# Queries and keys of an attention unit in four transfers, both heads together, in place of eight

## The chip, the core and the metric

The kernel runs on one core of one Trainium2 chip, in one launch. The metric is the device time of an execution in microseconds. Three runs of the kernel before gave 2951.26, 2949.39 and 2949.75 us, a median of 2949.75 us. A fourth execution was recorded by the hardware profiler; every view below is of that one.

## What is computed

One decoder layer on 2048 tokens of width 1024, in float32. Cut to the part that the change touches, with 64 columns per head, 8 heads of each kind:

```python
proj = h @ w_in[l]                                   # h: normalised, modulated tokens
q_f, k_f, v_f, q_s, k_s, v_s, f_logit = jnp.split(proj, offsets, axis=-1)
o_fox = forgetting_attention(...)                    # softmax(q.k/8 + F[t] - F[s]) v, s <= t
o_sb = stick_breaking_attention(...)                 # sigmoid(z) * prod(1 - sigmoid(z)) v, s < t
mix = jnp.concatenate([head_rms_norm(o_fox, ...), head_rms_norm(o_sb, ...)], axis=-1)
x = x + gate_a * (mix @ w_out[l])                    # then a gated MLP and a last norm
```

## The kernel before, in words

Products run on TensorE with each float32 operand split into a coarse part and a rest (`split`, L44 to L46, writes both), so a product is two or three matmuls.

The attention works in 32 **units** in a fixed order: first the stick-breaking kind (`sb`), then the forgetting kind (`fox`); in each, four pairs of heads; in each pair, four blocks of 512 queries. A unit's work grows with its block: block 0 of a `fox` pair is short, block 3 long. Two things run side by side in program order, mixed by `interleave`: `attend` for unit i (logits at L596 and L597, transposes of the weights at L606, their split copies at L610 and L611, the weighted values at L615), and `project`, which runs ahead and makes the queries, keys and values of later units.

A projection (`proj`) loads eight tiles `hp` of 512 KB, one for each 128 rows of the width, from DRAM (`hs`, L468), multiplies them with the query and key weights (L342), and writes the split queries and keys of the unit to DRAM (`qk_...`, L380 and L394). Every other pair also makes values (L413), which go to DRAM as `vs_...` (L440). There are ten `hp` buffers. They are also used for the loads of the late modulation (L776) and of the output weights (L746, L753), which run in the same stretch.

When unit i+1 is projected, `load_unit` brings its tiles from DRAM to SBUF while unit i is attended. `Q` is 128 partitions by 2 heads by 2 parts by 512 queries; the 64 columns of a head stand on partitions 0 to 63 and again on 64 to 127. `K` is 128 partitions by 2 heads by 512 keys; its lower 64 partitions hold the coarse part and its upper 64 the rest. A matmul over all 128 partitions thus sums two products. In DRAM the unit is `src`, 128 rows (head, then column) by 2 (queries, keys) by 2 parts by 512, so a row is 8 KB. There are two `Q` buffers and five each of `K` and `V`: the queries of unit i+1 can be fetched only when the last logits of unit i-1 are done, while keys of a pair stay for all its later blocks.

Nearly all transfers of this part, in and out, are issued by the SP queue, one after another: a transfer that waits (for a buffer, or for data) holds back all that stand behind it. The SP transfers take eight semaphores in turn, and each also waits until the transfer that used its semaphore before has landed. The order of the instructions on each engine is set by the scheduler of the framework before the run; the program gives it only the dependences and a few fixed places.

Of the kernel before, what the change touches and what calls it, by code (L numbers as in the profile page):

```python
# [21 lines left out]
HD = 64  # L22
# [12 lines left out]
def kernel(ctx: ExitStack, tc: tile.TileContext, x, c, w_ada, b_ada, g_attn, w_in, b_fgate,  # L35
                      g_out_fox, g_out_sb, w_out, g_mlp, w_up, conv_w, conv_b, w_down, g_final, out):
    nc = tc.nc
# [3 lines left out]
    def f(t):  # L41
        return t.bitcast(F32)
# [179 lines left out]
    rows = sm.tile([NR, P], F32, name="rows")  # L222
    begin_block(0)
    for r, src in ((R_GA, g_attn), (R_GM, g_mlp), (R_GF, g_out_fox), (R_GS, g_out_sb), (R_BA, b_ada)):
        n = src.shape[1] // P
# [121 lines left out]
    def unit_tiles():  # L347
        Q = sb.tile([P, 2, 2, TB], F32R, name="Q", tag="Q", bufs=2)
        K = sb.tile([P, 2, TB], F32R, name="K", tag="K", bufs=5)
        V = sb.tile([P, 4, 2, P], F32R, name="V", tag="V", bufs=5)  # L350
        return Q, K, V

    def load_unit(kind, p, tb, res):
        if (kind, p) == ("sb", 0):
            return
        Q, K, V = unit_tiles()
        src = qs.pop((kind, p, tb))
        for h in range(2):
            rows = slice(h * HD, (h + 1) * HD)
            for r in range(2):  # L360
                half = slice(r * HD, (r + 1) * HD)
                nc.sync.dma_start(f(Q[half, h]), src[rows, 0])
                nc.sync.dma_start(f(K[half, h]), src[rows, 1, r])
        nc.sync.dma_start(f(V), vs[kind][p][tb])
        res.append((Q, K, V))

# [459 lines left out]
    def attend_steps(u):  # L826
        kind, p, tb = u
        if kind == "fox":
            return sum(2 * (2 + 2 * tb + j2 + 1) for j2 in range(2)) + 1
        return sum(2 * (tb + 1 + 2 * tb + j2 + 1) for j2 in range(2)) + 1  # L830
# [189 lines left out]
    weights["sb", 0], results["sb", 0] = load_w("sb", 0), []  # L1020
    first_block(weights["sb", 0])
    load_unit(*units[0], results["sb", 0])
    loaded_units = [1]
    close_pool("mod")
# [5 lines left out]
    for i, u in enumerate(units):  # L1030
# [10 lines left out]
        n = attend_steps(u)  # L1041
# [16 lines left out]
        def follow(m):  # L1058
            while projected[0] < goals[min(m, n - 1)]:
                with tc.issue_after(marks[max(0, len(marks) - 1 - LAG)]) if START <= i < ENDQ else nullcontext():  # L1060
                    if next(ahead, 1) is not None:
                        break
            if nxt and projected[1] > i + 1 and loaded_units[0] == i + 1:
                loaded_units[0] += 1
                load_unit(*nxt, results[nxt[:2]])
# [10 lines left out]
    def chunk(u, c):  # L1076
        t, n, q = ORDER.get(u, TURN)[c]
        if (t, n) not in banks:
            banks[t, n] = bank(psc, "bc", 2) if u == 1 and t == 0 else bank(psd, "o", 4)
        with fixed():  # L1080
            out_matmuls(u, banks[t, n], t, n, q)
        return t, n, q
# [213 lines left out]
    for u in range(1, NU):  # L1296
        for c in range(8 if u == 1 else 0, 16):
            t, n, q = chunk(u, c)
# [386 lines left out]
    for i in range(7):  # L1685
        nxt = {}
        kept = []
        for s in range(2):
# [4 lines left out]
            if left:  # L1693
                half, n = lefts[i]
# [68 lines left out]
```

## Time and profile before

| | |
|---|---|
| median of 3 runs | 2949.75 us |
| the profiled execution, its own time | 2943.39 us |
| its span, first to last instruction | 2941.4 us |
| TensorE busy in the span | 2867.8 us (97%) |
| VectorE, ScalarE, GpSimd busy | 2179.5, 1686.0, 901.1 us |
| moved by the DMA engines | 601.89 MB, mean 205 GB/s |
| attention units | about 220 to 1480 us of the span |
| gated MLP, end | about 1480 to 2941 us |

The span is read as a sequence of stages. A view of groups gives the busy time of an engine by source line; the view of waits says which instruction waited, and for whom; the view by stretches gives for any piece of the span the busy time of each engine, the granted TensorE clock (PEclk, 1.00 is full), the busy share of the DMA engines, and the GB/s that they moved. PE is the matmuls of TensorE, DVE VectorE, ACT ScalarE, POOL GpSimd, SP the queue that issues transfers. Tiles are named without their buffer numbers, with the line of the kernel before.

### The profile page before, as it was taken

The numbers are of one execution on the slowest core, as the hardware profiler recorded it, in microseconds if no ns is written. First come the engines' busy times: TensorE is split into PE (matmuls) and PEld (weight loads), VectorE is DVE, ScalarE is ACT, GpSimd is POOL, SyncE is SP. The second block draws the span as 40 slices with busy tenths as digits, with TensorE's granted clock in tenths as the row PEclk, the third lists the DMA queues.
The fourth block names the chain that finished last, engine by engine and source line by source line (L and its number), as shares of the span: only waits on it lengthen the run. The fifth ranks groups of instructions, "written<-read, shape, count | busy, mean of one in ns | idle before, by whom it ended". The sixth has DMA issues, their size and how long they took to land.

```text
span 2941.4 us, 45922 instructions
## 1 busy us (share of the span) xinstructions
PE 2867.8 (97%) x15772; PEld 2459.7 (84%) x15772; DVE 2179.5 (74%) x3464; ACT 1686.0 (57%) x3187; POOL 901.1 (31%) x967
## 2 busy tenths in 40 slices
PE   8999999999999999999999999999999999999998
PEld 7888888888988988888888788888788888888887
DVE  5787778877886656658843788888998888575476
ACT  5776767677776656658744554444444445433342
POOL 0431322243032423231213344444254543142200
PEclk8999999999999999999999999999999999999999
DMA  9749756867469794794537775554754444975644
GB/s 293 255 139 321 236 188 207 301 211 229 162 212 356 269 277 139 232 323 140 182 120 233 245 232 128 130 136 129 236 132 125 130 130 132 309 257 185 216 158 151
DMA packets 348346, 601.89 MB, mean 205 GB/s; under 512 B 34672, under 2 KB 178800, under 8 KB 348112
## 3 DMA queue, kind: packets, MB, share of 16 engines
q1 hardware_dynamic: 324208, 558.06, 57.7%
q0 software_dynamic: 10880, 20.97, 4.3%
q10 hardware_dynamic: 13024, 19.93, 1.9%
q8 instruction: 124, 2.03, 0.3%
q14 instruction: 110, 0.90, 0.1%
HBM read 420.77 MB, written 177.02 MB: 203 GB/s over the span
## 4 chain that ended last, share of the span: by engine, by line
PE 46%; DMA 3%; DVE 2%; SPq 1%; ACT 1%; issue 1%; POOL 0%; DVEq 0%; ACTq 0%; POOLq 0%
PE ps_o L1315 19%; PE ps_t L1315 7%; PE ps_o L1614 6%; PE ps_t L1614 3%; PE ps_bc L1614 3%; PE ps_o L912 1%; PE ps_pv L615 1%; DMA r<-rstd 1%; PE ps_bc L912 1%; PE ps_pt L606 1%; PE ps_o L1609 1%; DMA wo<-wos 1%; DMA hm<-hf_m 1%; SPq L895 1%; DVE op L46 1%
## 5 line engine op out<-in xcount | busy, mean ns | idle before, releaser
L1315 PE MATMUL ps_o<-op,wu 128*128 128x512 f32 x2592 | 608.0, 389 | 2.0 <-DVE snap L1366 1.5
L1315 PEld LDWEIGHTS ps_o<-op,wu 128*128 128x128 f32 x2592 | 486.2, 188 | 103.9 <-DVE snap L1366 1.9
L611 DVE TENSOR_TENSOR at<-ps_pt,at 128x512 fp32r<-128x512 f32 (+1 forms) x576 | 366.1, 652 | 100.2 <-ACT at L610 97.3
L636 DVE TENSOR_TENSOR_SCAN a<-r,a 128x512 f32<-128x512 f32 (+2 forms) x320 | 368.3, 1167 | 77.8 <-ACT a L631 39.9
L342 PE MATMUL ps_pj<-hp,w_qk 128*128 128x512 f32 x1512 | 411.2, 403 | 14.5 <-DMA hp<-hs 12.9
L610 ACT ACTIVATE at<-ps_pt 128x512 fp32r<-128x512 f32 (+1 forms) x576 | 318.5, 576 | 139.1 <-PE ps_pt L606 123.1
L615 PE MATMUL ps_pv<-at,V 128*128 128x256 f32 x2216 | 386.8, 292 | 9.3 <-DVE at L611 4.2
L615 PEld LDWEIGHTS ps_pv<-at,V 128*128 128x128 f32 x2216 | 320.9, 190 | 39.8 <-DVE at L611 11.4
L342 PEld LDWEIGHTS ps_pj<-hp,w_qk 128*128 128x128 f32 x1512 | 275.4, 190 | 71.0 <-DMA hp<-hs 16.2
L45 ACT ACTIVATE wu<-wuraw 128x512 fp32r<-128x512 f32 x204 | 128.9, 632 | 248.5 <-PE ps_o L1315 190.1
L596 PE MATMUL ps_qk<-K,Q 128*128 128x512 f32 (+2 forms) x640 | 265.7, 416 | 5.6 <-ACT a L631 3.3
L413 PE MATMUL ps_pj<-w_v,hp 128*128 128x256 f32 (+1 forms) x1536 | 236.6, 288 | 2.1 <-DVE hp L422 1.6
L597 PE MATMUL ps_qk<-K,Q 128*128 128x512 f32 (+2 forms) x640 | 235.7, 369 | 0.0
L1315 PE MATMUL ps_t<-op,wu 128*128 128x512 f32 x888 | 220.8, 390 | 1.0 <-DVE op L46 1.0
L413 PEld LDWEIGHTS ps_pj<-w_v,hp 128*128 128x128 f32 x1536 | 209.0, 189 | 10.9 <-DVE q L373 1.5
L630 ACT ACTIVATE r<-ps_qk 128x512 f32<-128x512 f32 (+2 forms) x320 | 173.1, 541 | 58.2 <-PE ps_qk L597 55.5
L46 DVE TENSOR_TENSOR wu<-wuraw,wu 128x512 fp32r<-128x512 f32 x204 | 189.6, 930 | 18.1 <-ACT wu L45 16.7
L1315 PEld LDWEIGHTS ps_t<-op,wu 128*128 128x128 f32 x888 | 166.4, 188 | 36.5 <-DVE op L46 1.8
L606 PE MATMUL ps_pt<-edge,a 128*128 128x128 f32 x1088 | 185.1, 274 | 8.4 <-DVE a L636 7.8
L1614 PE MATMUL ps_o<-op 128*128 128x512 f32 x840 | 191.5, 389 | 0.0
L1614 PEld LDWEIGHTS ps_o<-op 128*128 128x128 f32 x840 | 157.7, 188 | 32.7
L679 ACT ACTIVATE p<-p,mn 128x128 f32<-128x128 f32 (+15 forms) x128 | 153.9, 1203 | 53.3 <-DVE mn L675 52.2
(342 smaller groups left out, 5237.6 us busy)
## 6 DMA issues: line engine op xcount, KB each, us to landing
hp<-hs SPq DMA_DIRECT2D x224, 512.0 KB
wuraw<-in_w_up_dram SPq DMA_DIRECT2D x80, 512.0 KB
ra<-g SPq DMA_DIRECT2D x136, 256.0 KB
rb<-in_w_down_dram SPq DMA_DIRECT2D x108, 256.0 KB
g<-u SPq DMA_DIRECT2D x80, 256.0 KB
hs<-hp SPq DMA_DIRECT2D x32, 512.0 KB
hp<-in_w_ada_dram SPq DMA_DIRECT2D x32, 512.0 KB
qk_fox<-q SPq DMA_DIRECT2D x32, 512.0 KB
```

The lines of the kernel that those rows point to most:

```text
L46: (lo_engine or nc.gpsimd).tensor_sub(lo, src, f(hi))
L342: nc.tensor.matmul(acc, w[kt][:, a, n], h[:, bb], start=kt == 0 and i == 0, stop=kt == KT - 1 and i == 2)
L413: nc.tensor.matmul(av[:, t * width:(t + 1) * width], hts[kt][:, a, tok], w[1][kt][:, bb, 0:width], start=kt == 0 and m == 0, stop=kt == KT ...
L596: nc.tensor.matmul(b[:, :cw], Q[:, hl, 0, qcols], K[:, hl, :cw], start=True, stop=False)
L597: marks.append(nc.tensor.matmul(b[:, :cw], Q[:, hl, 1, qcols], K[:, hl, :cw], start=False, stop=True).ins)
L606: nc.tensor.transpose(b[:, i * P:(i + 1) * P], blk(kts[kk], qi), ident)
L610: copies = [nc.scalar.activation(at[:, 0, lo:], b[:, lo:], AF.Copy).ins, nc.vector.tensor_sub(at[:, 1, lo:], b[:, lo:], f(at[:, 0, lo:])).ins]
L611: nc.vector.tensor_sub(at[:, 1, lo:], b[:, lo:], f(at[:, 0, lo:])).ins]
L615: m = nc.tensor.matmul(o[:, 0:2 * P], V[kt // 4][:, kt % 4, hl, :], rhs, start=first and kk == 0 and w == 0, stop=last and kk == 1 and w == 1)
L636: nc.vector.tensor_tensor_scan(rev, r[:, 0:need][:, ::-1], rev, 0.0 if right[qi] is None else right[qi][:, 0:1], ALU.mult, ALU.add)
L1315: nc.tensor.matmul(b, w[:, p, j], o[:, q], start=first and i == 0, stop=last and i == 2, skip_group_check=True)
L1614: nc.tensor.matmul(b, a[:, p, t * P:(t + 1) * P], w[:, q], start=first and i == 0, stop=last and i == 2, skip_group_check=True)
```

## The change

Only `load_unit` changes. For a unit, the kernel before issues four transfers for `Q` (256 KB each, one head onto one half of the partitions) and four for `K` (128 KB each). The changed kernel issues two for each, one for each half of the partitions, that carry both heads: 512 KB and 256 KB, with three-dimensional patterns (64 partitions, 2 heads, one contiguous run). The program text names the keys first. The bytes, the contiguous runs (4 KB for Q, 2 KB for K) and the destinations stay as they were. 28 of the 32 units load this way, so 224 transfers become 112.

```diff
-        for h in range(2):
-            rows = slice(h * HD, (h + 1) * HD)
-            for r in range(2):
-                half = slice(r * HD, (r + 1) * HD)
-                nc.sync.dma_start(f(Q[half, h]), src[rows, 0])
-                nc.sync.dma_start(f(K[half, h]), src[rows, 1, r])
+        for r in range(2):
+            half = slice(r * HD, (r + 1) * HD)
+            nc.sync.dma_start(f(K[half]), src[:, 1, r].rearrange("(h d) n -> d h n", h=2))
+        for r in range(2):
+            half = slice(r * HD, (r + 1) * HD)
+            nc.sync.dma_start(f(Q[half]), src[:, 0].rearrange("(h d) s n -> d h s n", h=2))
         nc.sync.dma_start(f(V), vs[kind][p][tb])
```

The scheduler sees other transfers, and so it also orders other instructions anew. On TensorE the order is the same up to about 239 us of the span of before; it differs by places of up to about 7 us of matmul work from there to about 480 us and from 800 to about 1340 us, and is the same again behind that, through the whole MLP. Three places follow. In a name such as `qk_fox_1_9353` the first number is the block of 512 queries, and `hs_2` is the third of the eight `hp` tiles of a projection.

**First place, SP, at the change from the `sb` units to the `fox` units.** The Q transfer here is that of block 1 of the first `fox` pair. Before (the next row is the load of `hs_2`):

```order
L440 DMA vs_fox_3_217<-q_10929 128x1024
L753 DMA wos_175<-hp 256x1x512
L746 DMA hp<-in_w_out_dram 128x1024
L363 DMA K<-qk_fox_3_10634 64x512
L753 DMA wos_175<-hp 256x1x512
L364 DMA V<-vs_fox_1_215 128x1024
L363 DMA K<-qk_fox_3_10634 64x512
L440 DMA vs_fox_3_221<-q_10930 128x1024
L363 DMA K<-qk_fox_3_10634 64x512
L362 DMA Q<-qk_fox_1_9353 64x1024 x4
L363 DMA K<-qk_fox_3_10634 64x512
L364 DMA V<-vs_fox_2_216 128x1024
```

And in the change, from the same point of the program:

```order
L746 DMA hp<-in_w_out_dram 128x1024
L753 DMA wos_175<-hp 256x1x512
L440 DMA vs_fox_3_217<-q_10877 128x1024
L360 DMA K<-qk_fox_3_10582 64x2x512
L753 DMA wos_175<-hp 256x1x512
L440 DMA vs_fox_3_221<-q_10878 128x1024
L360 DMA K<-qk_fox_3_10582 64x2x512
L364 DMA V<-vs_fox_1_215 128x1024
L468 DMA hp<-hs_2_62 128x1024
L363 DMA Q<-qk_fox_1_9309 64x2x1024 x2
L468 DMA hp<-hs_3_63 128x1024
L753 DMA wos_176<-hp 256x1x512
```

The load of `hs_2` and the last quarter of the keys of block 3 have moved ahead of the queries of block 1; the `V` of block 2 has moved behind them.

**Second place, TensorE, at the first logits of that unit** (block 1 of the first `fox` pair). Before, they are the second pair of L596 and L597 in these rows:

```order
L606 MATMUL ps_pt<-edge,p 128x128 x3
L596 MATMUL ps_qk<-K,Q 128x512
L597 MATMUL ps_qk<-K,Q 128x512
L596 MATMUL ps_qk<-K,Q 128x512
L597 MATMUL ps_qk<-K,Q 128x512
L615 MATMUL ps_pv<-at,V 128x256
L606 MATMUL ps_pt<-edge,p 128x128 x4
L615 MATMUL ps_pv<-at,V 128x256 x3
L716 MATMUL ps_pt<-headsel,sq 128x2 x2
```

In the change they are again the second pair:

```order
L596 MATMUL ps_qk<-K,Q 128x512
L597 MATMUL ps_qk<-K,Q 128x512
L615 MATMUL ps_pv<-at,V 128x256
L606 MATMUL ps_pt<-edge,p 128x128 x2
L342 MATMUL ps_pj<-hp,w_qk 128x512 x6
L615 MATMUL ps_pv<-at,V 128x256 x3
L606 MATMUL ps_pt<-edge,p 128x128 x5
L716 MATMUL ps_pt<-headsel,sq 128x2 x2
L596 MATMUL ps_qk<-K,Q 128x512
L597 MATMUL ps_qk<-K,Q 128x512
```

Between the last logits of block 0 and the first of block 1 now stand six projection matmuls (those of `hs_2`), four of L615, seven of L606 and two of L716.

**Third place, SP, ahead of the third `fox` pair**, where keys, sums and queries of its blocks are fetched together. Before:

```order
L468 DMA hp<-hs_4_72 128x1024
L363 DMA K<-qk_fox_1_11941 64x512 x4
L363 DMA K<-qk_fox_2_12345 64x512
L653 DMA Fb<-fs 128x1024
L363 DMA K<-qk_fox_2_12345 64x512 x3
L653 DMA Fb<-fs 128x1024
L362 DMA Q<-qk_fox_1_11941 64x1024 x4
L440 DMA vs_fox_0_222<-q_13722 128x1024
L440 DMA vs_fox_0_226<-q_13723 128x1024
L363 DMA K<-qk_fox_3_12746 64x512 x4
L468 DMA hp<-hs_5_73 128x1024
```

And in the change (`hs_2` stands directly ahead of these rows, as `hs_2` and `hs_3` stand ahead of those of before):

```order
L360 DMA K<-qk_fox_1_11877 64x2x512 x2
L468 DMA hp<-hs_3_71 128x1024
L360 DMA K<-qk_fox_2_12281 64x2x512
L653 DMA Fb<-fs 128x1024
L360 DMA K<-qk_fox_2_12281 64x2x512
L360 DMA K<-qk_fox_3_12678 64x2x512 x2
L653 DMA Fb<-fs 128x1024
L363 DMA Q<-qk_fox_1_11877 64x2x1024 x2
L440 DMA vs_fox_0_222<-q_13646 128x1024
L468 DMA hp<-hs_4_72 128x1024
L440 DMA vs_fox_0_226<-q_13647 128x1024
L468 DMA hp<-hs_5_73 128x1024
```

`hs_4` has moved from the front of the group to behind the queries and one store; `hs_5` still follows the same transfers as before.

## The prediction

> **What bounds the kernel now.** The page first: how long the span is, how much of it TensorE works, and what the chain that ended last is made of.
>
> ```profile
> span 2941.4 us, 45922 instructions
> PE 2867.8 (97%) x15772; PEld 2459.7 (84%) x15772; DVE 2179.5 (74%) x3464; ACT 1686.0 (57%) x3187; POOL 901.1 (31%) x967
> PE 46%; DMA 3%; DVE 2%; SPq 1%; ACT 1%; issue 1%; POOL 0%; DVEq 0%; ACTq 0%; POOLq 0%
> ```
>
> TensorE is the bound. It is idle for 73.6 us in all, and no change of a load can win more than the part of these that lies where the load runs. Next the busy time by stretches; columns are the stretch, its length, the busy time of each engine (instructions), the granted clock, the DMA share and GB/s.
>
> ```profile
> 220.00:480.00 260.00, 256.58 (x1672) 229.14 (x1672) 206.20 (x270) 187.45 (x401) 57.69 (x75) 1.00 0.69 234
> 480.00:800.00 320.00, 308.15 (x2018) 272.73 (x2017) 250.53 (x330) 232.73 (x520) 92.04 (x120) 1.00 0.70 228
> 800.00:1340.00 540.00, 524.13 (x3429) 470.01 (x3428) 361.43 (x851) 351.23 (x690) 168.44 (x218) 0.99 0.76 254
> 1340.00:1480.00 140.00, 134.48 (x923) 117.02 (x923) 119.47 (x322) 108.80 (x205) 30.32 (x55) 1.00 0.51 161
> ```
>
> In these attention stretches PE is idle for 3.4, 11.9, 15.9 and 5.5 us, 36.7 us together. The change reorders TensorE's work only in the first and the third (19.3 us idle); behind them every order is as before. Which idle time belongs to a transfer, the waits of PE between 220 and 1480 us say (total, times, longest):
>
> ```profile
> PE ps_pj L342 <- DMA hp<-hs: 12.9, 8, 6.0
> PE ps_pt L606 <- DVE a L636: 6.1, 14, 1.1
> ```
>
> No row of that view names Q, K or V of a loaded unit. So the transfers that the change touches never make PE wait by themselves; they can do so only by what stands behind them in SP's queue, the `hp` loads, which cost 12.9 us.
>
> **The change part by part.** *Issue time on SP.* These rows give count and minimum, median and maximum ns of an issue:
>
> ```profile
> L362 SPq DMA_DIRECT2D Q<-qk_fox x64: 444/587/892, 787.2 to 1401.2; - x64
> L363 SPq DMA_DIRECT2D K<-qk_fox x64: 444/541/1122, 676.1 to 1371.2; - x64
> L316 SPq DMA_DIRECT2D raw_qk<-in_w_in_dram x56: 368/404/1691, 42.0 to 1154.8; - x56
> L316 SPq DMA_DIRECT2D raw_v<-in_w_in_dram x24: 327/328/757, 320.4 to 999.4; - x24
> ```
>
> Removed: 112 Q and 112 K issues, 112 x 0.587 + 112 x 0.541 = 126 us of SP. Added: 112 issues of a three-dimensional form that the trace does not show for 64 partitions. Its price lies between one old issue (0.54 us) and two (1.17 us); the nearest pair of rows, three against two dimensions at 128 partitions, is 0.404 against 0.328, so I take 0.57 x 1.23 = 0.70, or 78 us. SP saves some 48 us (0 to 66). What hides it: SP mostly stands waiting.
>
> ```profile
> SPq L362 <- PE ps_qk L597: 60.3, 13, 15.6
> SPq L468 <- DMA Q<-qk_fox: 10.5, 15, 1.5
> ```
>
> The first row is the wait of Q for its buffer, 60.3 us, which stays with one transfer or four. The second is the `hp` loads waiting for a Q transfer eight places ahead to land; fewer places are taken now, but the bytes ahead of an `hp` are the same. Of PE's 12.9 us, 6.0 and 3.4 us are two single waits; the 6.0 is the third place, below, and the 3.4 is this one:
>
> ```profile
> PE ps_pj L342 <- DMA hp<-hs: 3.4, 1, 3.4
> 1226.92 5.59 SPq L776 DMA_DIRECT2D hp<-in_w_ada_dram  x2
> 1232.60 5.36 SPq L468 DMA_DIRECT2D hp<-hs  x8
> ```
>
> There the `hp` loads stand behind two modulation loads (5.59 us), and still do in the change. That leaves 12.9 - 6.0 - 3.4 = 3.5 us that SP's freed time could reach: **-1 us** (-3.5 to 0).
>
> *The rate of a Q transfer.* SP issued the four of one unit alone; the stretches say what moved then, and, for comparison, under eight `hp` loads of 128 partitions.
>
> ```profile
> 787.24 2.37 SPq L362 DMA_DIRECT2D Q<-qk_fox  x4
> 789.00:790.00 1.00, 1.00 (x11) 1.00 (x10) 1.00 (x2) 0.59 (x1) 0.00 (x0) 1.00 1.09 246
> 791.00:792.00 1.00, 1.00 (x11) 1.00 (x10) 0.99 (x3) 1.00 (x5) 0.14 (x1) 1.00 1.07 250
> 747.00:760.00 13.00, 13.00 (x84) 11.45 (x83) 10.68 (x17) 9.28 (x22) 0.59 (x2) 1.00 1.00 363
> ```
>
> The DMA engines are full in all three, yet Q moves at 246 to 250 GB/s and `hp` at 363. A transfer into half of the partitions is slower by the byte. The change keeps bytes and halves but stays twice as long in one half. Bounds: the 250 stays (0), or it falls to half of 363, 182 GB/s. 28 units x 1.57 MB = 44 MB; 44/0.250 = 176 us of transfer, 44/0.182 = 242, so up to 66 us more, nearly all beside other work. I take 250, **0 us** (0 to +7, a tenth of the 66 reaching PE).
>
> The Trainium skill (SBUF — State Buffer, "Door 1: The DMA port swizzle") says that partitions 0 to 63 reach only 8 of 16 ports, about 218 GB/s. The trace agrees that a half is slower, but shows 246 to 250 with alternating halves; by 218 throughout the 44 MB would take 26 us more.
>
> *First place: Q of block 1 of the first `fox` pair.* Both heads now come in each transfer, so the first logits wait for all of Q (1 MB) where half of it was enough; at 250 GB/s the other 0.52 MB is 2.1 us.
>
> ```profile
> 866.16 3.23 SPq L362 DMA_DIRECT2D Q<-qk_fox  x4
> SPq L468 <- DMA Q<-qk_fox: 3.5, 4, 1.1
> 877.37 0.32 SPq L468 DMA_DIRECT2D hp<-hs  x1
> 877.03 0.39 PE L596 MATMUL ps_qk<-K,Q 128*128 128x512 f32 x1
> 855.00:877.00 22.00, 17.22 (x106) 13.80 (x105) 18.43 (x38) 18.14 (x41) 9.48 (x12) 1.00 1.02 309
> 863.31 1.52 PE L342 MATMUL ps_pj<-hp,w_qk 128*128 128x512 f32 x6
> 867.67 0.60 PE L606 MATMUL ps_pt<-edge,a 128*128 128x128 f32 x4
> 878.65 0.50 PE L716 MATMUL ps_pt<-headsel,sq 128*128 128x2 f32 x4
> ```
>
> The wait row is of 870 to 878.5 us: each of four `hp` loads went out when one of the four Q transfers had landed, the last at 877.37. The first logits ran at 877.03, before all of Q was there. In the change 4096 KB stand ahead of Q from the same point where it were 3456 KB: 0.66 MB at the 309 GB/s of this stretch, 2.1 us, so Q is complete at 879.5. But six L342 (1.4 us until the next can start), four L606 (0.45) and the two L716 (0.35) now run ahead of those logits, 2.2 us: PE comes there at 879.2. **+0.3 us** (0 to +4.2, both delays with no cover).
>
> *Third place.* Before, the chain of 20 transfers ended in the longest wait:
>
> ```profile
> 1045.92 2.54 SPq L468 DMA_DIRECT2D hp<-hs  x3
> 1052.80 2.93 PE L342 MATMUL ps_pj<-hp,w_qk 128*128 128x512 f32 x6 [6.01 <-DMA hp<-hs]
> 1035.00:1045.00 10.00, 10.00 (x77) 9.37 (x75) 5.42 (x11) 5.53 (x12) 0.41 (x1) 1.00 1.03 243
> 1046.00:1053.00 7.00, 0.99 (x5) 0.55 (x5) 1.77 (x7) 2.58 (x9) 1.60 (x3) 0.86 1.03 337
> 1050.00:1060.00 10.00, 7.20 (x27) 6.02 (x28) 1.54 (x4) 2.41 (x6) 1.05 (x3) 0.66 1.04 293
> ```
>
> The DMA engines were full (1.03), so `hs_5` came at 1052.80 because of bytes, not of issues. Counted from `hs_2`, 5632 KB stand ahead of it before and after. But `hs_4`, which came early before, now stands 1 MB ahead of `hs_5`: at 337 GB/s it lands 3.1 us sooner, at 1049.7. PE reaches its wait without the six matmuls of `hs_4` (1.4 us), at 1045.4, and waits 4.3 us; the six and the logits behind them then cover the way to 1052.8. 4.3 for 6.0: **-1.7 us** (-6 to +3). The granted clock fell to 0.66 behind the wait: 10 us at that clock cost up to 3.4 us more, on either side of the change.
>
> *The other new orders*, from 239 to 480 and 800 to 1340 us. The 19.3 us idle there, less the 9.4 of the two long waits, leave 9.9 us that can go or come: **0 us** (-5 to +10; a new wait can be as long as the longest, 6.0, with its clock, 3.4).
>
> Sum: -1 + 0 + 0.3 - 1.7 + 0 = -2.4 us. Against the profiled execution's own 2943.39 us (2.0 us around the span) that is 2941.0; that execution ran 6.4 us below the median of the runs, 2949.75, and on the median's scale the forecast is 2947.4, said as **2947.5 us**.
>
> **The rivals.**
>
> *Slower: queries late at the short blocks.* Block 0 of a pair is attended in about 11 us, and Q of block 1 can be fetched only when Q's other buffer is free. If PE reaches the first logits less than 2.1 us after the first head landed, it waits for the second head. For it: the first place, with no time to spare. Against it: the view of waits shows none for Q, and the new order puts 2.2 us of work in between. It decides where that cover is late itself (`hs_2` now has to land first). Price at four `fox` pairs: 4 x (2.1 + 2.1) = 16.8 us at most, 10 us with cover at some: 2959.5.
>
> *Slower: half the ports.* The longer run in one half falls toward 182 GB/s, and later `hp` loads come later: 7 us, 2956.5. For it: 250 against 363. Against it: the old order alternated only each 256 KB, and stayed at 250.
>
> *Faster: SP was the brake.* If the `hp` waits come of issue and places in the queue, all but the 3.4 us go, 9.5 us, with 3.4 us of clock: 2937. For it: the 10.5 us of `hp` loads behind Q. Against it: full DMA engines at the longest wait. The Trainium skill (SBUF — State Buffer, "The DMA setup-cost knee") gives every transfer a fixed cost of roughly 2 us; by that, 112 fewer would take 224 us less on the queues, this rival taken further. The trace speaks against it: four Q in a row move at 246 to 250 GB/s without a gap. What chance it has is inside this rival's.
>
> **How the numbers follow.** 0.2%, 5.9 us, is about what a measurement of this kernel can tell from no change; the forecast lies inside. Chances: forecast 0.50; late queries 0.21; half the ports 0.06; SP the brake 0.18; other orders beyond 5.9 us, 0.02 faster and 0.03 slower. So faster 0.20, within 0.50, slower 0.30. The forecast's own case is 2943.9 to 2955.6, 0.2% around the median of before. To leave out no more than two in ten the range goes to 2937 (SP the brake) and 2963 (late queries, near its 16.8): 2937 to 2963.
>
> **What would show it.** Right: an issue of the new Q form near 0.7 us; the GB/s of a Q alone still near 250; PE's wait for `hp` ahead of the third `fox` pair some 4 us, in place of 6; no row of waits with Q or K; idle time in 800 to 1340 us near 14 us. Late queries would show as waits of L596 on Q of 2 us or more at block 1 of the `fox` pairs; half the ports as Q at 220 GB/s or less. An idle time in 800 to 1340 us above 25 us, or long new waits of L342 on `hp` with a clock below 0.9 behind them, would make the prediction wrong.

## The result, and the profile after

The changed kernel takes **2964.06 us** (median of 5 runs, 2958.68 to 2975.42) where the kernel before takes 2949.39 (2948.72 to 2951.26): a ratio of 1.0055, 95% interval 1.0043 to 1.0066. It is slower by some 15 us. The forecast of 2947.5 was wrong, and so was its sign; the median lies 1.1 us above the range.

The page of the changed kernel, the same two lines as were read of before:

```profile
span 2957.0 us, 45806 instructions
PE 2875.3 (97%) x15772; PEld 2467.7 (83%) x15772; DVE 2172.7 (73%) x3464; ACT 1689.3 (57%) x3187; POOL 898.1 (30%) x967
```

Of the 15.6 us by which the span grew, 8.1 are idle time of TensorE (81.7 us for 73.6) and 7.5 busy time of the same 15772 matmuls, at a granted clock of 0.989 for 0.993. One profile each is thin ground: that of before is of an execution 6.4 us below the median, and three kernels below that cost nothing (`wait_whole_q`, `eight_by_half`, `q_in_four_both_heads`) show 73 to 79 us idle and 2873 to 2878 us busy. So the stages are read one by one. Two of the four stretches again (length, busy time of each engine, granted clock, DMA share, GB/s):

```profile
480.00:800.00 320.00, 307.07 (x2007) 273.01 (x2006) 247.05 (x330) 233.64 (x521) 90.67 (x120) 0.99 0.71 227
800.00:1340.00 540.00, 517.37 (x3358) 465.11 (x3356) 348.95 (x816) 343.79 (x675) 166.72 (x214) 0.97 0.78 253
```

The second of them is idle for 22.6 us where it was 15.9, with the clock at 0.97 for 0.99; the other two are idle for 4.2 and 6.5 us, where it was 3.4 and 5.5. What PE waited for between 220 and 1480 us (total, times, longest):

```profile
PE ps_pj L342 <- DMA hp<-hs: 15.4, 6, 5.9
PE ps_pt L606 <- DVE a L636: 10.8, 14, 3.5
...
PE ps_qk L596 <- DMA Q<-qk_fox: 0.4, 1, 0.4
```

The waits for `hp` grew from 12.9 to 15.4 us, those of the transposes L606 for DVE from 6.1 to 10.8. Q itself is waited for once, 0.4 us. Two rows test terms of the prediction directly: the issue time of the new forms (minimum, median, maximum ns), and a Q that moves alone, microsecond by microsecond:

```profile
L363 SPq DMA_DIRECT2D Q<-qk_fox x32: 573/580/632, 790.3 to 1415.5; - x32
L360 SPq DMA_DIRECT2D K<-qk_fox x32: 573/580/1272, 680.4 to 1380.4; - x32
```

```profile
792.00:793.00 1.00, 1.00 (x10) 1.00 (x10) 1.00 (x2) 0.63 (x2) 0.00 (x0) 1.00 1.02 287
793.00:794.00 1.00, 1.00 (x11) 1.00 (x10) 1.00 (x3) 0.37 (x2) 0.00 (x0) 1.00 1.06 225
794.00:795.00 1.00, 1.00 (x11) 1.00 (x10) 0.99 (x3) 1.00 (x6) 0.08 (x1) 1.00 1.01 217
795.00:796.00 1.00, 1.00 (x11) 1.00 (x10) 0.86 (x3) 0.94 (x3) 0.51 (x2) 1.00 1.04 209
```

An issue costs 0.58 us, less than the 0.70 of the forecast, and SP still gains nothing for PE. Q moves at 209 to 225 GB/s in three of the four microseconds, where before showed 246, 229 and 250. From its first issue to its last landing this Q takes 7.7 us, where before it took 7.0.

**Where most of the time goes.** Between 1150 and 1250 us PE waits for `hp` twice, and in each half of this stretch it gets through fewer matmuls (the count behind the first busy time), at a lower clock. After:

```profile
PE ps_pj L342 <- DMA hp<-hs: 9.4, 2, 5.9
1150.00:1200.00 50.00, 45.90 (x282) 39.94 (x281) 33.86 (x89) 30.78 (x52) 11.94 (x18) 0.93 0.38 111
1200.00:1250.00 50.00, 42.55 (x303) 39.44 (x302) 27.52 (x71) 29.85 (x65) 13.99 (x22) 0.90 0.80 233
```

And before, where the waits for `hp` in these 100 us came to 3.9:

```profile
1150.00:1200.00 50.00, 49.32 (x346) 43.97 (x345) 44.64 (x116) 37.71 (x66) 9.93 (x18) 1.00 0.38 107
1200.00:1250.00 50.00, 46.29 (x314) 42.36 (x313) 29.10 (x77) 32.08 (x72) 18.60 (x25) 0.93 0.84 276
```

The two waits end at 1167.82 us (3.53 us, a new one) and at 1218.85 us (5.87, where before waited 3.40). Behind each the granted clock is 0.50 over 5 us (0.51 behind the one of before), and 0.72 and 0.71 over 10 us. From these, an estimate: the lower clock costs up to 2.8 and 2.9 us more.

**One place read to its end.** At 497.49 us PE waits 3.49 us for DVE; before, no wait there passed 0.5 us. The chain goes back through DVE and POOL to a transfer. SP's queue, before and after (start, duration):

```profile
475.35 0.54 SPq L451 DMA_DIRECT2D vd<-xt  x1
...
482.25 0.37 SPq L457 DMA_DIRECT2D xt<-vd  x1
```

```profile
477.18 0.37 SPq L451 DMA_DIRECT2D vd<-xt  x1
...
487.51 0.37 SPq L457 DMA_DIRECT2D xt<-vd  x1
```

The read L457 must wait until the write L451 has landed: 6.9 us from issue to issue before, 10.3 us after. The `hp` and K transfers that stand ahead of the write are the likely reason; this was not tested by itself. POOL, before and after, and then PE after:

```profile
487.27 2.57 POOL L458 TENSOR_TENSOR xt<-xt 128x1024 f32<-128x1024 f32 x1 [16.36 <-DMA xt<-vd]
```

```profile
491.86 2.45 POOL L458 TENSOR_TENSOR xt<-xt 128x1024 f32<-128x1024 f32 x1 [18.54 <-DMA xt<-vd]
...
495.64 0.29 POOL L633 TENSOR_SCALAR_AFFINE_SELECT a<-a 128x128 f32<-128x128 f32 x1
```

```profile
497.49 0.33 PE L606 MATMUL ps_pt<-edge,a 128*128 128x128 f32 x1 [3.49 <-DVE a L636]
```

POOL works in order. Its subtraction L458 starts 4.6 us later, of which 1.8 stood already when the write was issued; the mask L633 stands behind it, DVE's scan needs the mask, and PE's transposes need the scan. No view of Q, K or V names this: a transfer was late that the change doesn't touch.

### The profile page after: what moved, and what is told of

It is laid out like the page before. It is cut to its first block, busy times and chain, and to the rows that moved or that the text cites. A ratio compares the mean times of both kernels' runs of the same rounds, so it can differ in the third digit from the quotient of the medians.

```text
span 2957.0 us, 45806 instructions
## 1 busy us (share of the span) xinstructions
PE 2875.3 (97%) x15772; PEld 2467.7 (83%) x15772; DVE 2172.7 (73%) x3464; ACT 1689.3 (57%) x3187; POOL 898.1 (30%) x967
## 4 chain that ended last, share of the span: by engine, by line
PE 78%; DMA 10%; DVE 4%; issue 3%; ACT 2%; POOL 2%; SPq 0%; DVEq 0%; ACTq 0%; POOLq 0%
PE ps_o L1315 19%; PE ps_pj L342 8%; PE ps_t L1315 7%; PE ps_pv L615 6%; PE ps_o L1614 6%; PE ps_pt L606 5%; PE ps_pj L413 5%; PE ps_o L912 5%; PE ps_t L1614 3%; PE ps_bc L1614 3%; PE ps_qk L596 3%; PE ps_qk L597 3%; DMA hp<-hs 2%; DMA hp<-in_w_ada_dram 1%; PE ps_bc L912 1%
## 5 line engine op out<-in xcount | busy, mean ns | idle before, releaser
L342 PE MATMUL ps_pj<-hp,w_qk 128*128 128x512 f32 x1512 | 413.8, 405 | 18.7 <-DMA hp<-hs 15.4
L615 PE MATMUL ps_pv<-at,V 128*128 128x256 f32 x2216 | 387.6, 292 | 10.0 <-DVE oT L738 4.3
L615 PEld LDWEIGHTS ps_pv<-at,V 128*128 128x128 f32 x2216 | 323.4, 191 | 39.5 <-DVE at L611 10.1
L596 PE MATMUL ps_qk<-K,Q 128*128 128x512 f32 (+2 forms) x640 | 266.9, 417 | 5.7 <-ACT a L631 2.8
L597 PE MATMUL ps_qk<-K,Q 128*128 128x512 f32 (+2 forms) x640 | 236.6, 370 | 0.0
L46 DVE TENSOR_TENSOR wu<-wuraw,wu 128x512 fp32r<-128x512 f32 x204 | 189.9, 931 | 18.0 <-ACT wu L45 16.7
L606 PE MATMUL ps_pt<-edge,a 128*128 128x128 f32 x1088 | 187.0, 276 | 13.0 <-DVE a L636 12.5
```

The lines of the kernel that those rows point to most:

```text
L46: (lo_engine or nc.gpsimd).tensor_sub(lo, src, f(hi))
L342: nc.tensor.matmul(acc, w[kt][:, a, n], h[:, bb], start=kt == 0 and i == 0, stop=kt == KT - 1 and i == 2)
L596: nc.tensor.matmul(b[:, :cw], Q[:, hl, 0, qcols], K[:, hl, :cw], start=True, stop=False)
L597: marks.append(nc.tensor.matmul(b[:, :cw], Q[:, hl, 1, qcols], K[:, hl, :cw], start=False, stop=True).ins)
L606: nc.tensor.transpose(b[:, i * P:(i + 1) * P], blk(kts[kk], qi), ident)
L615: m = nc.tensor.matmul(o[:, 0:2 * P], V[kt // 4][:, kt % 4, hl, :], rhs, start=first and kk == 0 and w == 0, stop=last and kk == 1 and w == 1)
```

## The experiments

Two things changed at once: the form of the transfers, and with it the order in which the scheduler put every engine's work. To take them apart, some kernels hold each engine's instructions in a given order, by edges that only fix the order of issue:

```
for a, b in zip(order[engine], order[engine][1:]):
    tc.add_manual_dep(b, a.name, NoSync)
```

The edges themselves cost nothing that can be told: `wait_whole_q`, which is the kernel before with these edges and a few waits more, takes +1 us. "Old order" is that of before, "new order" that of the change. All kernels do the whole computation; where the load has fewer or more lines, later line numbers shift by a few. The ratio is that of the single runs on record, and can stand a little off the quotient of the two medians; the last column is the ratio less 1, times 2950 us.

| kernel | median us (before, same chip) | ratio, 95% interval | by the ratio, us |
|---|---|---|---|
| the change | 2964.06 (2949.39) | 1.0055 (1.0043 to 1.0066) | +16 |
| four_old_order | 2960.98 (2949.36) | 1.0042 (1.0030 to 1.0054) | +12 |
| four_old_early | 2964.38 (2950.83) | 1.0037 (1.0024 to 1.0049) | +11 |
| eight_new_order | 2975.37 (2949.36) | 1.0079 (1.0064 to 1.0093) | +23 |
| q_in_two | 2966.14 (2949.36) | 1.0064 (1.0049 to 1.0079) | +19 |
| k_in_two | 2963.34 (2949.36) | 1.0049 (1.0031 to 1.0066) | +14 |
| q_in_two_old_order | 2962.93 (2953.52) | 1.0039 (1.0026 to 1.0053) | +12 |
| q_in_two_again | 2955.56 (2948.53) | 1.0023 (1.0012 to 1.0034) | +7 |
| k_in_two_old_order | 2954.04 (2953.52) | 0.9997 (0.9983 to 1.0011) | -1 |
| eight_by_half | 2951.95 (2950.83) | 1.0006 (0.9992 to 1.0020) | +2 |
| wait_whole_q | 2949.53 (2948.71) | 1.0002 (0.9989 to 1.0015) | +1 |
| q_in_four_both_heads | 2949.93 (2948.53) | 1.0003 (0.9991 to 1.0014) | +1 |
| changed_hp_first | 2977.14 (2948.71) | 1.0091 (1.0076 to 1.0107) | +27 |
| by_head_old_order | 3572.63 (2950.83) | 1.2095 (1.2075 to 1.2115) | +618 |
| by_head_new_order | 3565.00 (2950.83) | 1.2071 (1.2051 to 1.2091) | +611 |
| pairs_old_order | 2924.99 (2953.52) | 0.9909 (0.9895 to 0.9924) | -27 |
| pairs_new_order | 2935.43 (2953.52) | 0.9950 (0.9937 to 0.9964) | -15 |

The theories: **A**, the new orders cost the time; **B**, the transfers do. Of B there are three forms. **G**: coarser transfers, the first logits must wait for a whole Q. **H**: a transfer into half of the partitions is the slow part, and long runs in one half slower still. **L**, which came later: a larger transfer lands later, and what stands behind it too.

### Order or transfers

**four_old_order.** The load lines are those of the change; each engine is held in the order of before.

> The four transfers of the change, with every engine's instructions held in the order that they have in the kernel before (each engine's instructions are chained in that order; where the two old transfers of a pair stood apart, the merged one stands at the later place). Only the form of the transfers differs from the kernel before. Theory A (the new orders of the engines cost the 14.7 us, the transfers themselves nothing): 2949 us, 2945 to 2953, and the wait of L342 on hp in 1100 to 1250 us is back to what it was (about 3.4 us once). Theory B (the transfers themselves cost it: whole queries needed, longer runs in one half): 2961 us, 2957 to 2966, with waits of L596 on Q.

**eight_new_order.** The load lines are those of before; each engine is held in the order of the change.

> The eight transfers of the kernel before, with every engine's instructions held in the order that they have in the changed kernel (the two old transfers of a pair stand where the merged one stands). Theory A (orders): 2964 us, 2959 to 2970, with the same waits of L342 on hp at 1167 and 1218 us as in the changed kernel. Theory B (transfers): 2950 us, 2946 to 2954.

2960.98 and 2975.37 us. Theory A fell in the first: the merged transfers alone, in an unchanged order, cost 12 us. Theory B fell in the second: the new order with the old transfers costs 23, 5 us above even A's range. The two don't add: together they are the change's +16. The old order is the better one with eight transfers, and no worse with four (+12 and +16, intervals that overlap). In the first, PE waits like this from 220 to 1480 us:

```profile
PE ps_pj L342 <- DMA hp<-hs: 17.0, 10, 6.6
...
PE ps_qk L596 <- DMA Q<-qk_fox: 2.0, 1, 2.0
```

With the order held, the waits for `hp` went from 12.9 to 17.0 us, and the one wait for Q is the first place of the prediction, without its new cover: 2.0 us. Of the second kernel, the same view:

```profile
PE ps_pj L342 <- DMA hp<-hs: 17.6, 10, 6.9
PE ps_pt L606 <- DVE a L636: 14.4, 13, 5.3
```

Its longest wait for DVE, 5.3 us, is the place at 497 us again, and between 1180 and 1300 us it waits 9.4 us for `hp`, as the change does. How long two pieces of the work take says it more sharply. The n-th matmul of PE is the same point of the work in all these kernels, where the matmuls before it are the same ones; the table gives the time between two such points, worked out from the starts of the matmuls. The third column has the four kernels in the old order that cost nothing (`k_in_two_old_order`, `eight_by_half`, `wait_whole_q`, `q_in_four_both_heads`).

| piece, in us of before | before | no cost | four_old_order | eight_new_order | the change |
|---|---|---|---|---|---|
| 480.1 to 500.1 (around the `vd` write) | 20.0 | 20.1 to 21.0 | 24.4 | 26.1 | 23.4 |
| 1085.6 to 1262.5 (the two `hp` waits) | 176.9 | 176.4 to 179.5 | 178.7 | 186.8 | 187.0 |

In the first piece time is lost with the four transfers in either order, and with the new order and eight. In the second, some 10 us of the change's loss, it is lost with the new order, with eight transfers as with four.

**four_old_early.** As four_old_order; of the two old places of a merged pair, the earlier one.

> As four_old_order (the four transfers of the change, every engine in the order of the kernel before), but a merged transfer stands at the earlier of the two old places, not at the later one. If the 11.6 us of four_old_order came of the later places of the keys: 2950 us, 2946 to 2953. If they came of the transfers' form (theories H and G): 2960 us, 2956 to 2965.

+11 us: not where the merged keys stand, but the transfers' form.

### Queries or keys

**q_in_two** and **k_in_two**, each with an order of its own:

```diff
-                nc.sync.dma_start(f(Q[half, h]), src[rows, 0])
+            nc.sync.dma_start(f(Q[half]), src[:, 0].rearrange("(h d) s n -> d h s n", h=2))
```

> Only the queries are merged (two transfers of 64 partitions x 2 x 1024), the keys stay in four. The engines' orders come out anew: a third set, unlike before and unlike the change. Theory A (orders): no forecast from the transfers; any time from 2942 to 2965, lost or won where its own order differs, and no wait of L596 on Q above 1 us. Theory B (transfers, of which the large queries are the costly ones): 2960 us, 2956 to 2965.

```diff
-                nc.sync.dma_start(f(K[half, h]), src[rows, 1, r])
+            nc.sync.dma_start(f(K[half]), src[:, 1, r].rearrange("(h d) n -> d h n", h=2))
```

> Only the keys are merged (two transfers of 64 partitions x 2 x 512), the queries stay in four. Again an order of its own. Theory A (orders): any time from 2942 to 2965, by its own order. Theory B (transfers, the queries the costly ones): 2949 us, 2946 to 2952.

+19 and +14 us; 2966 lies above both ranges for the first, and theory B's 2949 fell in the second. With orders free, the theories are not told apart: a merge of the keys alone puts another matmul into 1848 of PE's 15772 places (by tile names) and loses 14 us, as k_in_two_old_order shows, by its order alone.

**q_in_two_old_order** and **k_in_two_old_order**: the same two edits, held in the old order.

> Queries in two transfers, keys in four, every engine held in the order of the kernel before. Theory G, the first logits waiting for a whole Q: this part carries most of the 11.6 us of four_old_order: 2957 us, 2953 to 2961, with the wait of L596 on Q at 886 us. If the keys carry it (the writes behind them come late): 2950 us, 2947 to 2953.

> Keys in two transfers, queries in four, every engine held in the order of the kernel before. If the keys carry the 11.6 us of four_old_order: 2959 us, 2955 to 2963, with the late vd write at 487 us and PE's waits there. If the queries carry it: 2951 us, 2948 to 2954.

+12 and -1 us. The queries carry the cost; the keys alone cost nothing. The wait of L596 on Q that was named for the queries is in no row. And the two merges together are not simply the sum of their places: the `vd` piece of the table above takes 21.1 us with merged queries and 21.0 with merged keys, but 24.4 with both.

### What of a merged Q costs

**eight_by_half.** Eight transfers, both heads of one half first:

```diff
-        for h in range(2):
-            rows = slice(h * HD, (h + 1) * HD)
-            for r in range(2):
-                half = slice(r * HD, (r + 1) * HD)
+        for r in range(2):
+            half = slice(r * HD, (r + 1) * HD)
+            for h in range(2):
+                rows = slice(h * HD, (h + 1) * HD)
```

> The eight transfers of the kernel before, of the same size, and the order of everything else on every engine as before; only their sequence within a unit is changed: both heads of the lower 64 partitions first, then both of the upper 64, as the merged transfers have it, in place of alternating halves. Theory H (long runs in one half of the partitions move slower, 209 to 225 GB/s in place of 246 to 250 for a Q alone, and what stands behind them comes late): 2959 us, 2955 to 2964, a Q alone at 225 GB/s or less. Theory G (coarser transfers: the first logits need a whole Q, a merged K lands at once): 2950 us, 2947 to 2953, a Q alone at 246 to 250.

+2 us, not told from none. The sequence of halves, in transfers of 256 KB, is not the cost: H, as put there, fell. A Q alone takes 7.1 us here from first issue to last landing, as before (7.0).

**wait_whole_q.** Eight transfers, old order; the first logits of each loaded unit wait for both heads:

```diff
+        tc.add_manual_dep(first_logits, load_of_q_head_1.name, Sync)
```

> The kernel before with its eight transfers and its orders; added is only that the first logits of each loaded unit wait for the queries of both heads (all four Q transfers), as they must where Q is merged. Theory G (the wait for a whole Q is the cost): 2961 us, 2957 to 2965, with waits of L596 on Q at block 1 of the fox pairs. Theory L (the merged transfers themselves land later, and so does what stands behind them, hp and vd): 2952 us, 2949 to 2955, the wait costing at most 2 us at 877 us.

+1 us, and PE's view of waits has no row with Q. G fell. This kernel has the same orders and the same buffers as q_in_two_old_order; only the number and size of the Q transfers differ.

**q_in_four_both_heads**, and **q_in_two_again** beside it:

```diff
-                nc.sync.dma_start(f(Q[half, h]), src[rows, 0])
+                a = r * HD + q * 32
+                nc.sync.dma_start(f(Q[a:a + 32]), both[q * 32:(q + 1) * 32])
```

> Queries in four transfers of 256 KB as before, but each with both heads of 32 partitions, in place of one head of 64; keys as before; every engine in the order of the kernel before. If the size of a transfer is the cost (a larger one lands later and holds up what stands behind it): 2950 us, 2947 to 2954. If the form is (both heads in one transfer): 2960 us, 2956 to 2964.

> The kernel of q_in_two_old_order once more, to stand beside q_in_four_both_heads on one chip: 2961 us, 2957 to 2965, by either theory.

+1 and +7 us, again with the same orders and buffers; +7 is 2955.56, below the 2957 to 2965 that were named. Both heads in one transfer cost nothing at 256 KB; two of 512 KB do. What lands when supports L in its first half. A Q that moves alone (block 0 of the first `fox` pair), from its first issue to its last landing, takes 6.8 to 7.1 us in all seven profiles looked at with four Q transfers (that of before among them), 7.7 us in five with two of 512 KB and 8.1 in a sixth, and 5.5 in the two pairs kernels below. Over all 28 loaded units, most of them among other transfers, the spread is wider: from the first issue of a Q to its last landing the median is 8.97 us before, 9.18 in wait_whole_q and 8.87 in q_in_four_both_heads, but 9.44 and 10.07 in the two runs of q_in_two, 10.05 in four_old_order and 10.30 in the change. An `hp` load takes 7.55 us to land on the mean before, and 8.11 and 7.97 in the last two; but 7.67 and 7.72 in the two runs of q_in_two, hardly more than the 7.60 of eight_by_half, which costs nothing. So L's second half, what stands behind Q, is seen where queries and keys are both merged, and not for the queries alone.

Shown is that two transfers of 512 KB into halves land later, and cost more, than four of 256 KB. Size and number change together here, and with them which earlier transfer's semaphore each later one has to wait for; also, the four of 256 KB go into 32 partitions each and take the halves by turns. No run takes these apart, and why the larger ones land later is open.

### A place in the queue, or a buffer

The longest new wait of the change, 3.53 us at 1167.82 us, is for an `hp` load that now stands behind Q on SP:

```profile
1151.19 1.23 SPq L363 DMA_DIRECT2D Q<-qk_fox  x2
1152.52 6.47 SPq L316 DMA_DIRECT2D raw_qk<-in_w_in_dram  x3
1164.20 0.34 SPq L468 DMA_DIRECT2D hp<-hs  x1
```

**changed_hp_first** moves that load, in the changed kernel, ahead of the two Q rows.

> The changed kernel with its orders; one hp load, that of the wait at 1167 us, is moved on SP ahead of the two Q loads that it stood behind (five places earlier). If the place in the queue is the cause of that wait: 3 to 5 us less than the changed kernel, 2960 us, 2957 to 2962, and no wait of L342 on hp there. If the buffer is (the load waits for POOL to be done with a modulation row in the same buffer): the Q loads now stand behind that wait, nothing is gained, 2964 us or more, up to 2970, and the load goes out not before 1155 us.

2977.14 us: by the ratios some 11 us slower than the change, and above the 2970 that was named for the buffer. Its SP queue:

```profile
1159.49 0.33 SPq L776 DMA_DIRECT2D hp<-in_w_ada_dram  x1
1170.29 0.33 SPq L468 DMA_DIRECT2D hp<-hs  x1
1170.71 2.12 SPq L363 DMA_DIRECT2D Q<-qk_fox  x2
1172.88 9.12 SPq L316 DMA_DIRECT2D raw_qk<-in_w_in_dram  x4
```

and what SP and PE waited for there:

```profile
SPq L468 <- DMA hp<-in_w_ada_dram: 6.4, 1, 6.4
...
SPq L468 <- POOL hp L783: 4.0, 1, 4.0
```

```profile
PE ps_pv L615 <- ACT at L610: 7.8, 1, 7.8
PE ps_pj L342 <- DMA hp<-hs: 7.6, 3, 6.6
```

The load waits for its buffer, which holds a modulation row until POOL has used it. It can't go earlier; put first, it holds Q and the weights behind it, and a new wait of PE of 7.8 us appears. The wait's row named the late transfer rightly, and the neighbour in the queue was the wrong suspect: the view of what SP itself waits for, in the change from 1150 to 1170 us, tells it.

```profile
SPq L468 <- POOL hp L783: 3.4, 1, 3.4
```

### All partitions at once

If loads into a half are the slow part of both kernels, merging the other way must help: one transfer for each head, into all 128 partitions.

**by_head_old_order** and **by_head_new_order**:

```diff
+        for h in range(2):
+            rows = slice(h * HD, (h + 1) * HD)
+            nc.sync.dma_start(f(K[:, h]), src[rows, 1].rearrange("d r n -> r d n"))
+        for h in range(2):
+            rows = slice(h * HD, (h + 1) * HD)
+            nc.sync.dma_start(f(Q[:, h]), src[rows, 0].rearrange(
+                "d (r s) n -> r d s n", r=1).to_broadcast([2, HD, 2, TB]))
```

> Four transfers again, but merged the other way: one for each head, into all 128 partitions (both halves), every engine held in the order of the kernel before. Theory H: the restriction to a half is gone, a Q alone moves at some 350 GB/s, and what stands behind it comes earlier: 2944 us, 2938 to 2949. Theory G: the first logits need one transfer of head 0, as many bytes as before: 2950 us, 2947 to 2954. If merging by itself is the cost (fewer, larger transfers, fewer places in the queue): 2961.

> The same four transfers by head into all 128 partitions, with the engines' orders as they come out for them: an order of its own, unlike before and unlike the change. By theory H less is lost than in the change, whatever the order: 2950 us, 2940 to 2960. If new orders cost some 15 us whatever the transfers: 2960.

3572.63 and 3565.00 us. A Q that moves alone, and PE's waits from 220 to 2100 us, of the first:

```profile
790.00:792.00 2.00, 2.00 (x15) 1.83 (x14) 1.33 (x4) 1.66 (x6) 0.29 (x1) 1.00 0.12 49
792.00:794.00 2.00, 2.00 (x12) 1.67 (x11) 1.22 (x2) 0.17 (x1) 0.29 (x1) 1.00 0.13 53
```

```profile
PE ps_pj L342 <- DMA hp<-hs: 300.5, 27, 46.5
```

A DMA share of 0.12 to 0.13 is 2 of 16 engines: the source pattern is 2 x 64 x 1024, its slowest dimension is 2, and the transfer moves at 49 to 53 GB/s. The Trainium skill (DMA: Bandwidth & Descriptors, "Why a DMA increments its semaphore by 16 and not by 1") says that the number of engines is the largest up to 16 that divides the slowest dimension of both patterns; the 0.12 agrees.

**pairs_old_order** and **pairs_new_order** take 64 as the slowest dimension: row d goes to partitions 2d and 2d+1. Queries and keys of a unit are laid out alike, so the sum over partitions is the same.

```diff
+        for h in range(2):
+            nc.sync.dma_start(f(K[:, h]), src[h * HD:(h + 1) * HD, 1])
+        for h in range(2):
+            nc.sync.dma_start(f(Q[:, h]), src[h * HD:(h + 1) * HD, 0].rearrange(
+                "d (r s) n -> d r s n", r=1).to_broadcast([HD, 2, 2, TB]))
```

> Four transfers, one for each head, into all 128 partitions: row d of the source goes to partitions 2d and 2d+1 (queries twice, keys one half each), so that 64 source rows can be shared out, where by_head_old_order had two. Every engine is held in the order of the kernel before. If its 2 of 16 DMA engines were all that was wrong with by_head_old_order, the 600 us are gone: then by theory G (the first logits wait for the bytes of one head, as before) 2949 us, 2946 to 2953; by theory H (a transfer into half of the partitions is the slow part) 2944 us, 2938 to 2949, a Q alone above 300 GB/s; if any merging into four costs what four_old_order cost, 2961 us.

> The same four transfers by head, with the engines' orders as they come out for them (a third order). Theory A (orders cost): 2960 us, 2950 to 2975. Theories G and H: within 4 us of pairs_old_order.

2924.99 us in the old order, 2935.43 in one of its own: both beat both kernels, the first by 0.91% (0.76 to 1.05). No theory had foreseen so much: H comes nearest, and the first is 13 us below its range; the second is below that of A, and 10 us above the first, where G and H allowed 4. Busy time from its page, two microseconds of a Q alone, and PE's waits from 220 to 1480 us:

```profile
PE 2864.1 (98%) x15772; PEld 2459.5 (84%) x15772; DVE 2174.6 (74%) x3464; ACT 1685.7 (58%) x3187; POOL 904.9 (31%) x967
```

```profile
783.00:784.00 1.00, 1.00 (x11) 1.00 (x10) 1.00 (x2) 0.96 (x3) 0.00 (x0) 1.00 0.91 340
784.00:785.00 1.00, 1.00 (x11) 1.00 (x10) 1.00 (x3) 0.04 (x1) 0.00 (x0) 1.00 0.84 287
```

```profile
PE ps_pj L342 <- DMA hp<-hs: 3.6, 5, 1.9
```

Q moves at 287 to 340 GB/s, lands 7.41 us after its first issue (median of 28, 8.97 before), and the waits for `hp` fall from 12.9 to 3.6 us; that of 6.0 us at the third place is gone. The number of transfers is that of the change, the bytes too. The Trainium skill (SBUF — State Buffer, "Door 1: The DMA port swizzle") puts a half of the partitions at about 218 GB/s. The 209 to 225 of the change agree; the 229 to 250 of before, which takes the halves by turns, lie above it. With bytes, order and number of transfers the same, these runs and four_old_order differ in the partitions that a transfer goes to, and in carrying one head or two: 39 us between them, and 27 between these and the eight transfers of before.

## Why the prediction was wrong

**Two steps failed, both terms taken as 0 us: "The rate of a Q transfer" (0 to +7) and "The other new orders" (-5 to +10).**

*The rate of a Q transfer.* By the runs the merged Q transfers cost 7 to 12 us in an unchanged order (q_in_two_again, q_in_two_old_order), and all four transfers 12 us (four_old_order). The direction of the bound was right: a Q alone takes 0.7 us longer, over 28 units some 20 us of transfer (an estimate from that one Q). The step let a tenth of such time reach PE; by the runs a third to more than half of it did. It asked at what rate a Q moves, and not when it lands and what waits behind it. On the way to PE the runs show the `vd` write, which the prediction never looked at, and later `hp` loads, where queries and keys are both merged. With merged queries alone PE waits 14.0 and 11.3 us for `hp`, no more than kernels that cost nothing (11.5 to 16.7), so there the way to PE stays open.

*The other new orders.* Most of what the change loses lies at the two `hp` waits between 1085.6 and 1262.5 us, some 10 us, and the same order loses it with the eight old transfers too. On top of the four transfers the new order added only 3 us (2964.06 against 2960.98, intervals that overlap), so the term isn't one that can be added. The bound had named the mechanism, a new wait with its clock; the mean of nothing was the mistake. Four times of five the fresh order of a set of transfers came out slower than the old order held: +16 for +12, +19 for +7 to +12, +14 for -1, -15 for -27; with by_head, +611 for +618, it is not told. Of these, the third and the fourth are clear of their intervals, and so is eight_new_order, +23 for nothing.

**A row read wrongly.** The prediction set 3.4 us aside as a wait behind two modulation loads, issued at 1226.92 us. In the trace that wait ends at 1208.81 us, before these loads were issued. The load that PE waited for went out behind the keys and queries of the fourth `fox` pair:

```profile
1195.26 1.86 SPq L362 DMA_DIRECT2D Q<-qk_fox  x3
...
1200.74 0.33 SPq L468 DMA_DIRECT2D hp<-hs  x1
```

So it is a place of the same kind as the third, and in the change the wait there is the longest, 5.87 us (3.4 to 5.3 in the old-order kernels that cost nothing).

**Issue time on SP: -1 us (-3.5 to 0).** The issue itself came cheaper than taken, 0.58 us, so SP saved some 126 - 112 x 0.58 = 61 us. Nothing of it is seen at PE: the waits for `hp` rose by 2.5 us. SP was no brake.

**First place: +0.3 us (0 to +4.2).** Right for the wait: 0.4 us in the change, where the new order gives cover, and 2.0 in four_old_order, where it doesn't; the prediction had 2.1 us for the bytes of the second head. That this is not where the time goes, wait_whole_q shows.

**Third place: 4.3 us of wait in place of 6.0.** From 1000 to 1100 us the changed kernel shows

```profile
PE ps_pj L342 <- DMA hp<-hs: 5.4, 2, 5.2
```

The sign may be right and the size was not. One profile can't tell more: the old-order kernels that cost nothing show 3.9 to 8.5 us there.

**The rivals.** Late queries at the short blocks: the sign and nearly the time were right, the mechanism not; no row of L596 on Q passes 0.4 us in the change, and the added wait costs nothing. Half the ports: the fall to 209 to 225 GB/s that it named was there in three of four microseconds, and it had 0.06; of the rivals it came nearest. The sequence of halves was not the reason (eight_by_half); two large transfers in place of four were. SP the brake: the saved issues bought nothing. Of the signs named for a wrong prediction one came and one did not: a long new wait on `hp` with a clock below 0.9 behind it (3.53 us, 0.50), but 22.6 us idle in 800 to 1340 us, not over 25.

**Still open:** why a 512 KB transfer into 64 partitions lands later than two of 256 KB, by what way the merged queries alone reach PE, and why each new order cost what it did; changed_hp_first shows for one of the two waits only that the place in the queue is not the cause.

## What to carry to other kernels

Fewer transfers are not cheaper ones: ask into how many partitions a transfer goes, over how many engines its slowest dimension spreads it, and when it lands for what stands behind it. Here the same four transfers were worth +12 us into halves, +618 us with a slowest dimension of 2, and -27 us into all partitions with one of 64. Where a scheduler orders the work, hold the old order to see what an edit itself does: here the order that came out anew was never clearly better than the old one held. And read a late transfer back to what its own queue waited for before naming its neighbour as the cause.

## What the hardware showed that was not expected

A transfer whose slowest source dimension is 2 ran on 2 of 16 DMA engines, 49 to 53 GB/s, and gave no other sign than the DMA share of 0.12 to 0.13. With orders and buffers the same, two Q transfers of 512 KB cost 7 to 12 us, and four of 256 KB with the same bytes nothing that can be told. And a wait of PE costs more than its length: in ten of the profiles, between 220 and 1480 us, each of the 20 idle times of 3.4 us or more was followed by a granted clock of 0.50 to 0.70 over the next 5 us; behind the ten of 2.0 to 2.9 us it was 1.00 five times and 0.66 five times.
